# The first FFN of a two-layer diffusion backbone by quarter products, its hidden state through DRAM

## The chip, the cores and the metric

The kernel runs on one core of one Trainium2 chip. The metric is the device time of one execution in microseconds; lower is better. The core has TensorE (matrix products, accumulated in PSUM banks of 512 fp32 columns), VectorE, ScalarE, GpSimd, and DMA queues, all of whose transfers here are issued by SyncE. Each engine works off its own instructions in order and waits on semaphores for the others; so the order of the instructions on an engine, which the tile framework's scheduler sets when it compiles the program, decides what a waiting instruction holds up.

## The reference

Two layers over 1024 latent tokens and 256 context tokens of width 1024. Each layer has a mixer (attention and gating in layer 0, Fourier mixing and a gated linear scan in layer 1), whose result goes through an out projection, and a SwiGLU FFN of hidden width 2816. The change is about layer 0's FFN, which works on tokens and context, and about what stands directly ahead of it and behind it.

```python
# layer 0: ab_mixer, layer 1: cd_mixer; D_MODEL 1024, SEQ 1024, CTX_LEN 256, FFN_HIDDEN 2816, all float32
def swiglu(h, w_gate, w_up, w_down):
    return (jax.nn.silu(h @ w_gate) * (h @ w_up)) @ w_down
...
    for i in range(DEPTH):
...
        mod = (silu_c @ ada_w[i] + ada_b[i])[:, None, :]
        mod_c = (silu_cc @ ada_w[i] + ada_b[i])[None, None, :]
...
        x = x + g_m * y
        x = x + g_f * swiglu(modulate(rmsnorm(x, norm_ffn_w[i]), sh_f, sc_f), ffn_w_gate[i], ffn_w_up[i], ffn_w_down[i])
        if not last:
            ctx = ctx + gc_m * y_c
            ctx = ctx + gc_f * swiglu(modulate(rmsnorm(ctx, norm_ffn_w[i]), shc_f, scc_f),
                                      ffn_w_gate[i], ffn_w_up[i], ffn_w_down[i])
    return rmsnorm(x, final_norm_w)
```

## The kernel before

All matrix products are done in split precision: each fp32 operand is a sum of a high and a low part (`split`, lines 54 to 57: a cast on ScalarE, a subtraction on VectorE), and `mm3` (lines 46 to 51) issues three matmuls, high by high, high by low, low by high. Activations lie transposed, width on the partitions: eight tiles `xT` of 128 x 1280 (tokens 0 to 511 as block 0, 512 to 1023 as block 1, the context as columns 1024 to 1279), and the normed input of the FFN `hT` as pairs named `hh`, `hl`, with `hc` for their context columns. The hidden width is 22 tiles of 128; two of them are a pair.

**Layer 0's FFN** (`ffn`, from line 329) goes over the 22 hidden tiles. `weights` (line 334) loads and splits 1024 x 128 of the gate and of the up matrix. `up` (line 337) makes, block by block, the gates `pg` and ups in PSUM, the product of silu and up (lines 347, 348), and its split `hhi`, `hlo`. After every second tile, `down` (line 352) multiplies two hidden tiles with 256 rows of the down matrix into eight output tiles `dn` per block, each at once added to `xT` by `residual` (line 318), on four PSUM banks in turn (tags t, t, m, o). Gates, ups and downs so alternate, and the hidden state stays on chip. After each `up` a `tick` carries the background generator `ada` (from line 160) one step on: it loads 512 KB of the conditioning weights (`adaw`, with one buffer in this stage) and adds them, scaled, to `adaacc` on VectorE (line 185, 1024 wide); after each eighth load TensorE transposes the sum (`adat`, banks m and o) and VectorE reduces it (line 207).

Ahead of it, `out_proj` (line 767) goes block by block in the order 0, 1, context, loads its weights in four parts for the first block, keeps two parts in the ring and splits two again into other places, and adds each output to `xT`. The rms norm (`rstd` line 266, `norm` line 285) follows block by block: squares on ScalarE, their sum `sqacc`, a sum over the partitions by TensorE (`ss`), a power on GpSimd, a spread over the partitions by TensorE (`rbc`, line 263), eight tiles each of line 297 and, for the low part, line 306.

**Layer 1's FFN** works by quarters for all pairs but the first: `quad` (line 645) takes the tokens and the two tiles of a pair as a 2 x 2 block matrix, and gets the four results from seven products (`qp`) instead of eight, each 4 slices of 128 by 3 matmuls of 512 columns, with sums of `hT` that are made once beforehand (`Sums`, `norm_second`) and sums of weight quarters. `Feed` (line 533) makes the weight units: `quarters` (line 582) loads 2 x 512 KB, subtracts on GpSimd (line 588) and splits units of 512 x 128 into a ring of four. Results are put together by VectorE's adds (line 650). Each pair's gates, the downs of the pair before (`down_sums`, line 745) and its ups alternate. There, `Norm.add` (line 436) makes the squares beside the residuals of `out_proj`, and `norm_first` stands behind block 0.

Between the layers `spill` writes `xT` to DRAM (`xd`), and the next stage begins with products `va`.

## Time and profile before

| | us |
|---|---|
| three runs | 2811.56 to 2816.33, median 2816.05 |
| the profiled execution | 2814.21 |
| its span, first to last instruction | 2812.4 |
| TensorE busy | 2703.8 (96%) |
| VectorE busy | 1739.5 (62%) |
| ScalarE busy | 956.9 (34%) |
| GpSimd busy | 314.7 (11%) |
| layer 0's FFN, first gates to the last pair's downs | 735 to 1621 |
| layer 1's FFN by quarters | 2173 to 2749 |

The profile is of one execution, which took 1.8 us more than its span. Busy time of TensorE is from a matmul's start to its modelled end, and matmuls overlap, so what one costs in a stream is read from the starts in the timeline. TensorE's granted clock was 0.988 of 2.4 GHz in the mean over the span.

### The profile page before, as it was taken

The page shows a single profiled execution, that of the slowest core. Times are in us where ns is not written, and L with a number is a line of the kernel's source. Part 1 is how long each engine was busy: PE and PEld are TensorE (multiplying, and loading weights), DVE is VectorE, ACT ScalarE, POOL GpSimd, SP SyncE. Part 2 cuts the span into 40 slices and gives each one's busy share as a digit, 9 for nine tenths or more (in the row PEclk, how much of TensorE's full clock was granted, in tenths as well). Part 3 has the DMA queues.
Part 4 walks back from the last instruction along what each step waited for, and adds up shares of the span by engine and source line. Part 5 has one row for each costly group of instructions (what it writes and reads, how often), then busy time and mean ns, then how long its engine had stood idle before and what let it go on. Part 6 is the DMA issues. An engine that isn't in the chain of part 4 may idle for free. (4 is left out here: it accounts for less than half of the span.)

```text
span 2812.4 us, 38777 instructions
## 1 busy us (share of the span) xinstructions
PE 2703.8 (96%) x14687; PEld 2295.6 (82%) x14687; DVE 1739.5 (62%) x3090; ACT 956.9 (34%) x2058; POOL 314.7 (11%) x313
## 2 busy tenths in 40 slices
PE   8999899989999999999999999899999999999998
PEld 3889788777888888888888878788777888888887
DVE  5655677666674545546434374866677666667666
ACT  3442466554421111111111145565334222223222
POOL 0000122221100000000000020312002111212111
PEclk9999999999999999999999999999899999999999
DMA  8545655765142322213211143452550211111112
GB/s 307 160 134 154 184 161 160 221 197 168 53 122 66 90 60 83 83 53 98 73 48 45 31 137 104 122 169 65 169 180 24 64 57 45 46 60 53 61 53 83
DMA packets 263162, 298.52 MB, mean 106 GB/s; under 512 B 33416, under 2 KB 206145, under 8 KB 262977
## 3 DMA queue, kind: packets, MB, share of 16 engines
q1 hardware_dynamic: 262977, 296.06, 34.7%
q8 instruction: 116, 1.90, 0.3%
q14 instruction: 69, 0.57, 0.1%
HBM read 228.09 MB, written 64.49 MB: 104 GB/s over the span
## 5 line engine op out<-in xcount | busy, mean ns | idle before, releaser
L56 ACT CAST whi<-wraw 128x512 fp32r<-128x512 f32 (+2 forms) x309 | 235.4, 766 | 722.8 <-PE dn L50 413.9
L318 DVE SCALAR_TENSOR_TENSOR xT<-dn,mod,xT 128x512 f32<-128x512 f32 (+1 forms) x448 | 300.5, 685 | 127.7 <-PE dn L51 126.8
L57 DVE TENSOR_TENSOR wlo<-wraw,whi 128x512 fp32r<-128x512 f32 (+2 forms) x309 | 282.3, 916 | 136.5 <-ACT whi L56 135.1
L49 PE MATMUL dn<-hhi,whi 128*128 128x512 f32 (+1 forms) x896 | 328.0, 367 | 4.9 <-DVE xT L318 3.3
L50 PE MATMUL dn<-hlo,whi 128*128 128x512 f32 (+1 forms) x896 | 326.7, 365 | 0.0
L51 PE MATMUL dn<-hhi,wlo 128*128 128x512 f32 (+1 forms) x896 | 326.5, 365 | 0.0
L49 PE MATMUL pg<-hh,whi 128*128 128x512 f32 x688 | 268.6, 390 | 1.2 <-DVE sg L348 1.2
L51 PE MATMUL pg<-hh,wlo 128*128 128x512 f32 x688 | 268.5, 390 | 0.6 <-DVE wlo L57 0.6
L50 PE MATMUL pg<-hl,whi 128*128 128x512 f32 x688 | 267.9, 389 | 0.0
L185 DVE SCALAR_TENSOR_TENSOR adaacc<-adaw,cs,adaacc 128x1024 f32<-128x1024 f32 x140 | 175.0, 1281 | 112.8 <-DMA adaw<-in_ada_w_dram 110.2
L49 PEld LDWEIGHTS dn<-hhi,whi 128*128 128x128 f32 x896 | 168.9, 189 | 36.9 <-DVE xT L318 8.0
L51 PEld LDWEIGHTS dn<-hhi,wlo 128*128 128x128 f32 x896 | 168.9, 189 | 27.0
L50 PEld LDWEIGHTS dn<-hlo,whi 128*128 128x128 f32 x896 | 169.0, 189 | 26.6
L588 POOL TENSOR_TENSOR wraw<-wraw 128x512 f32<-128x512 f32 x80 | 113.9, 1424 | 499.3 <-DVE wlo L57 293.2
L347 ACT ACTIVATE sg<-pg 128x512 f32<-128x512 f32 (+1 forms) x66 | 34.6, 524 | 353.8 <-PE pg L51 353.8
L348 DVE TENSOR_TENSOR sg<-sg,pg 128x512 f32<-128x512 f32 (+1 forms) x66 | 39.2, 594 | 187.0 <-ACT sg L347 187.0
L51 PEld LDWEIGHTS pg<-hh,wlo 128*128 128x128 f32 x688 | 129.2, 188 | 28.3 <-DVE wlo L57 1.5
L49 PEld LDWEIGHTS pg<-hh,whi 128*128 128x128 f32 x688 | 129.2, 188 | 27.1 <-DVE sg L348 1.4
L50 PEld LDWEIGHTS pg<-hl,whi 128*128 128x128 f32 x688 | 129.2, 188 | 25.9
L277 POOL TENSOR_TENSOR sqacc<-sqacc,sq 128x512 f32<-128x512 f32 (+1 forms) x14 | 17.0, 1218 | 901.5 <-ACT sq L276 900.4
L1058 POOL TENSOR_SCALAR y<-y,sst 128x768 f32<-128x768 f32 (+2 forms) x80 | 71.9, 900 | 257.8 <-DVE sst L1057 129.3
L50 PE MATMUL pg<-hc,whi 128*128 128x256 f32 x344 | 96.8, 281 | 0.0
(653 smaller groups left out, 6644.2 us busy)
## 6 DMA issues: line engine op xcount, KB each, us to landing
adaw<-in_ada_w_dram SPq DMA_DIRECT2D x96, 512.0 KB, 3.8
wraw<-in_ffn_w_gate_dram SPq DMA_DIRECT2D x44, 512.0 KB, 3.6
wraw<-in_ffn_w_up_dram SPq DMA_DIRECT2D x44, 512.0 KB, 3.7
wraw<-in_ffn_w_down_dram SPq DMA_DIRECT2D x44, 512.0 KB, 3.9
wraw<-in_ab_w_in_dram SPq DMA_DIRECT2D x20, 512.0 KB, 5.9
xd<-xT SPq DMA_DIRECT2D x16, 640.0 KB, 6.2
xs<-xd SPq DMA_DIRECT2D x32, 256.0 KB, 3.2
xd<-xs SPq DMA_DIRECT2D x32, 256.0 KB, 3.0
```

What stands on the lines that cost most here:

```text
L49: nc.tensor.matmul(out, wh, xh, start=start, stop=False)
L50: nc.tensor.matmul(out, wh, xl, start=False, stop=False)
L51: nc.tensor.matmul(out, wl, xh, start=False, stop=stop)
L56: s.nc.scalar.copy(hi, src)
L57: (s.nc.gpsimd if eng == "pool" else s.nc.vector).tensor_tensor(lo, src, f32(hi), ALU.subtract)
L185: nc.vector.scalar_tensor_tensor(acc[:, v], w, c, acc[:, v], ALU.mult, ALU.add)
L277: (add or nc.vector).tensor_tensor(acc[:, :n], acc[:, :n], sq[:, :n], ALU.add)
L318: s.nc.vector.scalar_tensor_tensor(xT[k][:, o:o + n], ps, s.mod[l][:, 8 * vec + k, sel:sel + 1], xT[k][:, o:o + n], ALU.mult, ALU.add)
L347: nc.scalar.activation(sg[:, :n], pg[:, :n], AF.Silu)
L348: nc.vector.tensor_tensor(sg[:, :n], sg[:, :n], pu[:, :n], ALU.mult)
L588: sub = lambda out, x, y: feed.s.nc.gpsimd.tensor_tensor(out, x, y, ALU.subtract)
L1058: nc.gpsimd.tensor_scalar(y[:, :256 + xn], y[:, :256 + xn], st[:, 5:6], 1.0, ALU.mult, ALU.mult)
```

## The change

Layer 0's FFN is rewritten to work by quarters, in two phases.

- `out_proj` runs its blocks in the order 0, context, 1. Its weights stay in a ring of three buffers: four loads for the first block, and the first two parts loaded and split again later. Layer 1 uses the same code, so its own order of weights changes too (2, 4, 6, 0 for block 1 instead of 4, 6, 0, 2). `Norm.add` follows each residual. x1 is written to DRAM.
- PSUM changes to single banks for the products. The first hidden pair is multiplied plainly; then the sums are made.
- **Phase 1**: for the ten other pairs a quad of gates and a quad of ups. The context columns are multiplied `beside`, on the same weight units (`cp`, 256 columns); for this a quad has an eighth unit. The hidden pairs, 2.6 MB each, go to DRAM (`hd`), except the last.
- **Phase 2**: x1 is loaded again, into the places that held the sums and inputs, and the downs of all eleven pairs follow, the hidden pairs loaded two pairs ahead.
- The conditioning is done by `ada_half`, with 512-wide loads of 256 KB in two buffers and 112 ticks: 8 a pair in phase 1, 3 a pair in phase 2.
- The scratch ring of the norm has 8 buffers instead of 9, and `norm_second`'s sums reuse a tile.

The diff, cut to its core ("..." marks what is left out):

```diff
+def ada_half(s, a, l, vecs):
+    nc = s.nc
+    for m in vecs:
+        sums = s.adap.tile([P, 2, 8], F32, name="adasum", tag="adasum", bufs=1)
+        for hf in range(2):
+            acc = s.adap.tile([P, 2, 512], F32, name="adaacc", tag="adaacc", bufs=1)
+            for k in range(KT):
+                w = s.adap.tile([P, 512], F32, name="adaw", tag="adaw", bufs=2)
+                c0 = D * m + 512 * hf
+                nc.sync.dma_start(w, a["ada_w"][l, k * P:(k + 1) * P, c0:c0 + 512])
+                for v in range(2):
+                    c = s.cs[:, k, v + 2:v + 3]
+                    if k == 0:
+                        nc.scalar.mul(acc[:, v], w, c)
+                    else:
+                        nc.vector.scalar_tensor_tensor(acc[:, v], w, c, acc[:, v], ALU.mult, ALU.add)
+                if k < KT - 1:
+                    yield 1
+            for v in range(2):
+                pt = psum(s, "mo"[v], "adat")
+                for j in range(4):
+                    nc.tensor.transpose(pt[:, j * P:(j + 1) * P], acc[:, v, j * P:(j + 1) * P], s.ident)
+                nc.vector.tensor_reduce(sums[:, v, 4 * hf:4 * hf + 4], pt.rearrange("p (j q) -> p j q", j=4),
+                                        AX.X, ALU.add)
+            if hf == 0:
+                yield 1
+        nc.vector.tensor_tensor(s.mod[l][:, 8 * m:8 * (m + 1), :], sums.rearrange("p v c -> p c v"),
+                                s.adab[:, 48 * l + 8 * m:48 * l + 8 * (m + 1)].rearrange("p (c o) -> p c o", o=1)
+                                .to_broadcast([P, 8, 2]), ALU.add)
+        yield 1
...
+def norm_ctx(s, N, hT):
+    N.spread()
+    for k in range(KT):
+        N.tile(k, scratch(s)[:, :CT], hT)
...
+def quarters(w, j, ctx=False):
...
-        sub(t, t, b11)
+        if not ctx:
+            sub(t, t, b11)
         for b in (b11, b21):
             feed.unit(b)
+            yield 0
+        if ctx:
+            feed.unit(t)
+            sub(t, t, b11)
             yield 0
         feed.unit(t)
         sub(t, b22, t)
...
+def quad(s, feed, xs, u, out, done, ctx=None):
     nc = s.nc
     add = lambda out, x, y: nc.vector.tensor_tensor(out, x, y, ALU.add)
+    pc = [psum(s, "t", "cp")[:, :CT] for _ in range(2)] if ctx else None
+    def beside(w, x, half):
+        for k in range(4):
+            mm3(nc, pc[x], (w[0][:, k, :], w[1][:, k, :]), ctx[0](4 * half + k), k == half == 0, k == 3 and half == 1)
+        if half:
+            ctx[1](x, pc[x])
     def product(i):
-        hi, lo = feed.take()
+        w = feed.take()
         ps = psum(s, "s", "qp")
         for k in range(4):
-            mm3(nc, ps, (hi[:, k, :], lo[:, k, :]), xs(i, k), k == 0, k == 3)
+            mm3(nc, ps, (w[0][:, k, :], w[1][:, k, :]), xs(i, k), k == 0, k == 3)
+        if ctx and i in (1, 2, 3):
+            beside(w, *{1: (0, 0), 2: (0, 1), 3: (1, 1)}[i])
+        if i in (1, 2, 5, 7):
+            tick(s)
...
+    if ctx:
+        beside(feed.take(), 1, 0)
+        feed.ahead()
...
+        if self.store:
+            for dst, src in zip(self.store[x], self.h[y, x]):
+                self.s.nc.sync.dma_start(dst[:, o:o + n], f32(src))
...
+def down_sums(s, feed, xT, hs, l, blocks, behind=None):
+    order = [(c, y, o, n) for c in (0, 4) for y, (o, n) in enumerate(blocks)]
...
+        if c == 0:
+            tick(s)
...
+    todo = list(zip(blocks, ((0, 2, 4, 6), (2, 4, 6, 0), (4, 6, 0, 2))))
+    steps = [(blk, k0) for blk, ks in todo for k0 in ks]
+    ahead, after = {0: (0, 2, 4)}, {0: (6,), 4: (0,), 8: (2,)}
+    weights = lambda k: wslab(s, w[q0 * P:(q0 + nq) * P, k * P:(k + 2) * P], nq, 2 * P)
+    for i, (blk, k0) in enumerate(steps):
...
+        for k in ahead.get(i, ()):
+            kept[k] = weights(k)
...
+        if i < len(steps) - 2:
+            for k in after.get(i, ()):
+                kept[k] = weights(k)
+        for x in range(2):
+            residual(s, xT, k0 + x, blk, ps[x][:, :n], l, 2)
+            norms[blk].add(k0 + x)
+        if k0 == todo[i // 4][1][-1]:
+            behind(blk)
...
+def load_x1(s, xT, xd, blocks):
+    for o, n in blocks:
+        for k in range(KT):
+            s.nc.sync.dma_start(xT[k][:, o:o + n], xd[k][:, o:o + n])
...
+def load_hidden(s, hd, i):
+    hs = {}
+    for x in range(2):
+        t, c = ([f(s, p, 2 * i + x) for p in range(2)] for f in (hslot, cslot))
+        for p in range(2):
+            s.nc.sync.dma_start(f32(t[p]), hd[x][p][:, :T])
+            s.nc.sync.dma_start(f32(c[p]), hd[x][p][:, T:])
+        for y, (o, n) in enumerate(XBLK):
+            hs[y, x] = [u[:, o:o + n] for u in t]
+        hs[2, x] = c
+    return hs
...
+            place = lambda i, k: slot(s, k if i == 6 else 4 + k, (P, 2, 512), F32R, name="sums")
...
+            def behind(blk):
+                if blk == BLK[0]:
+                    norm_first(s, N[blk], hT, S)
+                    ws.append(early_weights(s, lambda i: ep.tile([P, 2, 512], F32R, name=f"e{i}"), wg))
+                elif blk == BLK[2]:
+                    norm_ctx(s, N[blk], hT)
+                else:
+                    spill(s, xT, xd[0])
+            out_proj(s, a["ab_w_out"][0], mix, xT, 0, [BLK[0], BLK[2], BLK[1]], [4, 5, 6, 7], N, behind)
+            single_banks(s, pps)
+            wps.close()
+            s.wp = wps.enter_context(R("wpf"))
+            fps = es.enter_context(ExitStack())
+            s.fp = fps.enter_context(R("fpf"))
+            pairs = range(2, HT, 2)
+            jobs = [whole(wu, 0)] + [quarters(w, j, True) for j in pairs for w in (wg, wu)]
+            order = [HT - 2] + list(range(0, HT - 2, 2))
+            feed = Feed(s, jobs + [rows(wd, j) for j in order])
+            ws.append(feed_whole(feed))
+            xs = lambda i, k: S.operand(hT, i, k)
+            ctx_ = lambda k: [h[:, T:TA] for h in hT[k]]
+            H = Hidden(s, ctx_, hd[0:2])
+            sums, rest = norm_second(s, N[BLK[1]], hT, S)
+            for y in (0, 2, 1):
+                H.plain(ws, hT, y)
+            sums()
+            rest()
+            nps0.close()
+            eps.close()
+            s.fh = fps.enter_context(R("fhf"))
+            s.adap = fps.enter_context(R("ad1"))
+            s.bg = chain(ada_half(s, a, 0, [5]), ada_half(s, a, 1, range(6)))
+            H.keep_all()
+            for j in pairs:
+                H = Hidden(s, ctx_, hd[j:j + 2] if j < HT - 2 else None)
+                H.gate(feed, xs)
+                H.up(feed, xs)
...
             xT = alloc_x(s)
...
+            load_x1(s, xT, xd[0], BLK)
+            hs = {HT - 2: H.h}
+            for i, j in enumerate(order):
+                for n in (0, 1, 2) if i == 0 else (i + 2,):
+                    if 0 < n < len(order):
+                        hs[order[n]] = load_hidden(s, hd[order[n]:order[n] + 2], n % 4)
+                down_sums(s, feed, xT, hs[j], 0, BLK)
+            drain(s)
+            acol(s, 1, 0)
+            acol(s, 1, 1)
+        wps.close()
+        s.wp = wps.enter_context(R("wp"))
+        double_banks(s, pps)
+        spill(s, xT, xd[1])
+        s.np_ = nps.enter_context(P_("np2", side="left"))
+        hT = alloc_hc(s)
```

On TensorE, in the gates of a later pair: each row is line, instruction, output <- inputs and shape; `hh` and `hl` are the two parts of the input, `whi` and `wlo` of a weight. Before, gates and ups of one block alternate on the same input:

```order
L49 MATMUL pg<-hh_514,whi 128x512
L50 MATMUL pg<-hl_515,whi 128x512
L51 MATMUL pg<-hh_514,wlo 128x512
L49 MATMUL pg<-hh_516,whi 128x512
L50 MATMUL pg<-hl_517,whi 128x512
L51 MATMUL pg<-hh_516,wlo 128x512
L49 MATMUL pg<-hh_516,whi 128x512
L50 MATMUL pg<-hl_517,whi 128x512
L51 MATMUL pg<-hh_516,wlo 128x512
```

After, the last slice of a quarter product `qp` and the first ones of the context product `cp` on the same weight unit:

```order
L51 MATMUL qp<-hh_516,wlo 128x512
L49 MATMUL qp<-hh_518,whi 128x512
L50 MATMUL qp<-hl_519,whi 128x512
L51 MATMUL qp<-hh_518,wlo 128x512
L49 MATMUL cp<-hc_528,whi 128x256
L50 MATMUL cp<-hc_529,whi 128x256
L51 MATMUL cp<-hc_528,wlo 128x256
L49 MATMUL cp<-hc_530,whi 128x256
L50 MATMUL cp<-hc_531,whi 128x256
```

What moved: the context columns, which had a pass of their own behind the two token blocks, now stand between the quarter products.

On VectorE, ahead of the first FFN: line 297 and 306 are the norm's tiles of block 0, line 318 the residuals of the out products `op`. Before, with the residuals of block 1:

```order
L306 SCALAR_TENSOR_TENSOR hl_513<-nt,mod_180,hh_512 128x512
L297 SCALAR_TENSOR_TENSOR nt<-xT_7780,acol_183,rbc 128x512
L297 SCALAR_TENSOR_TENSOR nt<-xT_7781,acol_183,rbc 128x512
L306 SCALAR_TENSOR_TENSOR hl_517<-nt,mod_180,hh_516 128x512
L318 SCALAR_TENSOR_TENSOR xT_7784<-op,mod_180,xT_7784 128x512
L297 SCALAR_TENSOR_TENSOR nt<-xT_7782,acol_183,rbc 128x512
L297 SCALAR_TENSOR_TENSOR nt<-xT_7783,acol_183,rbc 128x512
L318 SCALAR_TENSOR_TENSOR xT_7785<-op,mod_180,xT_7785 128x512
L306 SCALAR_TENSOR_TENSOR hl_521<-nt,mod_180,hh_520 128x512
```

After, where lines 418 and 427 are the norm's tiles and line 351 is the residual, now of the context (256 columns):

```order
L418 SCALAR_TENSOR_TENSOR a_7859<-xT_7782,acol_183,rbc 128x512
L427 SCALAR_TENSOR_TENSOR hl_517<-a_7859,mod_180,hh_516 128x512
L418 SCALAR_TENSOR_TENSOR a_7860<-xT_7783,acol_183,rbc 128x512
L418 SCALAR_TENSOR_TENSOR a_7860<-xT_7784,acol_183,rbc 128x512
L418 SCALAR_TENSOR_TENSOR a_7861<-xT_7785,acol_183,rbc 128x512
L427 SCALAR_TENSOR_TENSOR hl_521<-a_7860,mod_180,hh_520 128x512
L418 SCALAR_TENSOR_TENSOR a_7861<-xT_7786,acol_183,rbc 128x512
L427 SCALAR_TENSOR_TENSOR hl_525<-a_7861,mod_180,hh_524 128x512
L351 SCALAR_TENSOR_TENSOR xT_7783<-op,mod_180,xT_7783 128x256
```

What moved: residuals of the next block stood between the norm's tiles, and now stand behind the last of them; a weight subtraction of 1024 columns (`wlo`) stands just ahead of these tiles.

On TensorE, at the end of the first FFN, where the last pair's downs `dn` meet the next norm (`ss` its sums over the partitions, `rbc` its spread). Before, at block 0's sums:

```order
L51 MATMUL dn<-hhi,wlo 128x512
L50 MATMUL dn<-hlo,whi 128x512
L51 MATMUL dn<-hhi,wlo 128x512
L281 MATMUL ss<-ones,sqacc 128x1 x4
L49 MATMUL dn<-hhi,whi 128x512
L50 MATMUL dn<-hlo,whi 128x512
```

After, where `va` is the first product of the next stage:

```order
L49 MATMUL dn<-hc_15760,whi 128x256
L50 MATMUL dn<-hc_15761,whi 128x256
L51 MATMUL dn<-hc_15760,wlo 128x256
L314 MATMUL ss<-ones,sqacc 128x1 x8
L296 MATMUL rbc<-diag,ones 128x512
L314 MATMUL ss<-ones,sqacc 128x1 x2
L49 MATMUL va<-whi,hh_16449 128x272 x2
```

What moved: the sums and the spread of block 0 stood among the last pair's downs, and now stand behind the last of these, together with those of block 1 and the context (`x8`, `x2`).

## Rows read from the trace of the kernel before

**Rows 1.** Page, part 1: busy us of each engine, share, instructions

```profile
PE 2703.8 (96%) x14687; PEld 2295.6 (82%) x14687; DVE 1739.5 (62%) x3090; ACT 956.9 (34%) x2058; POOL 314.7 (11%) x313
```

**Rows 2.** Windows: busy us by engine, clock, DMA share, GB/s

```profile
735.00:1620.00 885.00, 881.02 (x4658) 758.18 (x4657) 439.44 (x580) 153.30 (x219) 3.84 (x6) 1.00 0.23 70
2173.00:2749.00 576.00, 576.00 (x2543) 476.95 (x2542) 392.61 (x542) 162.02 (x273) 108.78 (x76) 1.00 0.17 54
1621.50:1673.00 51.50, 45.41 (x260) 37.60 (x259) 38.31 (x57) 22.56 (x38) 18.97 (x16) 1.00 0.43 146
...
620.00:650.00 30.00, 26.32 (x163) 22.88 (x164) 21.83 (x66) 16.99 (x51) 5.26 (x7) 1.00 0.74 230
```

**Rows 3.** Waits of TensorE, 735 to 1621: total us, times, longest

```profile
PE dn L49 <- DVE xT L318: 1.4, 3, 0.9
PE pg L49 <- DVE sg L348: 1.2, 1, 1.2
```

**Rows 4.** Timeline of TensorE, 2172.9 to 2179: start us, duration, instruction

```profile
2173.00 0.39 PE L50 MATMUL qp<-mixc,whi 128*128 128x512 f32 x1
...
2175.72 0.39 PE L50 MATMUL qp<-mixd,whi 128*128 128x512 f32 x1
```

**Rows 5.** Timeline of TensorE, 1001.5 to 1004.6

```profile
1001.58 0.28 PE L49 MATMUL dn<-hhi,whi 128*128 128x256 f32 x1
...
1004.45 0.40 PE L49 MATMUL pg<-hh,whi 128*128 128x512 f32 x1
```

**Rows 6.** Groups of VectorE, 735 to 1620: count, busy us, mean ns, idle before

```profile
L185 DVE SCALAR_TENSOR_TENSOR adaacc<-adaw,cs,adaacc 128x1024 f32<-128x1024 f32 x98 | 123.0, 1281 | 99.1 <-DMA adaw<-in_ada_w_dram 98.9
...
L318 DVE SCALAR_TENSOR_TENSOR xT<-dn,mod,xT 128x256 f32<-128x256 f32 x80 | 36.9, 481 | 8.5 <-PE dn L51 8.5
L57 DVE TENSOR_TENSOR hlo<-sg,hhi 128x512 fp32r<-128x512 f32 x44 | 30.4, 690 | 23.4 <-ACT hhi L56 23.4
...
L207 DVE TENSOR_REDUCE adasum<-adat 128x4 f32<-128x512 f32 x28 | 18.6, 684 | 40.1 <-PE adat L206 40.1
...
L348 DVE TENSOR_TENSOR sg<-sg,pg 128x256 f32<-128x256 f32 x21 | 8.7, 414 | 0.0
```

**Rows 7.** Groups of VectorE, 2173 to 2749

```profile
L57 DVE TENSOR_TENSOR wlo<-wraw,whi 128x512 fp32r<-128x512 f32 x173 | 130.4, 754 | 58.5 <-ACT whi L56 57.2
L318 DVE SCALAR_TENSOR_TENSOR xT<-dn,mod,xT 128x512 f32<-128x512 f32 x157 | 117.5, 749 | 67.5 <-PE dn L51 67.4
L650 DVE TENSOR_TENSOR hu<-qp,hu 128x512 f32<-128x512 f32 x57 | 39.3, 689 | 43.3 <-PE qp L51 43.1
...
L738 DVE TENSOR_TENSOR g<-g,g 128x512 f32<-128x512 f32 x9 | 16.0, 1778 | 0.0
L738 DVE TENSOR_TENSOR hu<-hu 128x512 f32<-128x512 f32 x9 | 16.0, 1773 | 0.0
...
L738 DVE TENSOR_TENSOR g<-g,ua 128x512 f32<-128x512 f32 x18 | 12.4, 688 | 0.3
```

**Rows 8.** Group of GpSimd, 2173 to 2749

```profile
L588 POOL TENSOR_TENSOR wraw<-wraw 128x512 f32<-128x512 f32 x76 | 108.8, 1431 | 470.1 <-DVE wlo L57 271.4 <-DMA wraw<-in_ffn_w_up_dram 138.3 <-DMA wraw<-in_ffn_w_gate_dram 36.5
```

**Rows 9.** Waits of VectorE, 735 to 1620

```profile
DVE adaacc L185 <- DMA adaw<-in_ada_w_dram: 98.9, 39, 8.7
...
DVE hlo L57 <- ACT hhi L56: 26.2, 40, 0.7
```

**Rows 10.** Waits of TensorE, 2040 to the end

```profile
PE op L49 <- ACT nt L439: 4.9, 1, 4.9
PE ss L450 <- DVE nt L443: 2.4, 1, 2.4
PE pg L49 <- ACT nt L439: 1.6, 1, 1.6
```

**Rows 11.** Wait of TensorE, 1600 to 1680

```profile
PE rbc L263 <- DVE diag L260: 1.7, 1, 1.7
```

**Rows 12.** DMA issues on the page: count, KB each, us to landing

```profile
adaw<-in_ada_w_dram SPq DMA_DIRECT2D x96, 512.0 KB, 3.8
```

More of the change, by code (lines that the diff above doesn't have):

```diff
@@ L579, in ahead, with feed_whole @@
             next(self.gen, 0)
-def quarters(w, j):
+def feed_whole(feed):
+    units = [[u.rearrange("p k n -> p (k n)") for u in feed.take()] for _ in range(4)]
+    return [[units[2 * half + x] for half in range(2)] for x in range(2)]
+def quarters(w, j, ctx=False):
     loads = [w[512 * x:512 * (x + 1), j * P:(j + 2) * P].rearrange("(k p) n -> p k n", p=P) for x in range(2)]
@@ L1873, in body @@
         nps = ExitStack()
[L1874 to L1896 removed]
+        s.nbanks = "mo"
@@ L1947, in body @@
     feed = Feed(s, jobs + [rows(wd, HT - 2)])
-    units = [feed.take() for _ in range(4)]
-    ws.append([[[u.rearrange("p k n -> p (k n)") for u in units[2 * half + x]] for half in range(2)] for x in range(2)])
+    ws.append(feed_whole(feed))
     H = Hidden(s)
-    sums, rest = norm_second(s, norms_[XBLK[1]], hT, S)
+    sums, rest = norm_second(s, N[XBLK[1]], hT, S)
     H.plain(ws, hT, 0)
@@ L1958, in body @@
     s.fh = pool("fp3", side="right")
-    for y in range(2):
-        for x in range(2):
-            H.keep(y, x)
+    H.keep_all()
     xs = lambda i, k: S.operand(hT, i, k)
@@ L1965, in body @@
         H.gate(feed, xs)
-        down_sums(s, feed, xT, last.h, 1)
+        down_sums(s, feed, xT, last.h, 1, XBLK)
         H.up(feed, xs)
     sps.close()
-    down_sums(s, feed, xT, H.h, 1, final(s, pool("fin", side="left"), a, xT, out))
+    down_sums(s, feed, xT, H.h, 1, XBLK, final(s, pool("fin", side="left"), a, xT, out))
     dump("x4", xT, T)
```

254 lines of the change are left out of this document (95 added, 159 removed).

## The prediction

> **What bounds the kernel now.** I read the page first: TensorE is busy for 96% of the span [rows 1], so the first question is how many matmul columns go away, and the second is where TensorE will wait that does not wait today. The table of windows gives the stages. In the first FFN (735 to 1620 us) TensorE is busy for 881.0 of 885 us and VectorE for half of it; in the second FFN, which already uses quarter products, TensorE never stops while VectorE is at 392.6 of 576 us [rows 2]. The waits of TensorE in the first FFN are a few single microseconds, the longest 1.2 [rows 3]. So the stage is a pure matmul stream, and a matmul that is left out there is saved in full, as long as the work beside it keeps up. What a matmul costs is the step from start to start, not the printed duration (0.39 us, which overlaps): the twelve of 512 columns in the timeline go from 2173.00 to 2175.72 us, 0.2267 us each [rows 4], the 24 of 256 columns from 1001.58 to 1004.45 us, 0.120 us each [rows 5].
>
> **Products removed.** A pair of hidden tiles needs, per matrix, eight block products of 512 columns; by quarters it needs seven. A block product is 4 slices of the contraction by 3 matmuls, 12 matmuls. Ten of the eleven pairs, two matrices: 10 x 2 x 12 = 240 matmuls x 0.2267 = **-54.4 us**. Context columns cost the same 96 matmuls of 256 per pair as before, only spread over the quarter units, and the down products are all kept. A pair's gates and ups then take 168 x 0.2267 + 96 x 0.120 = 49.6 us instead of 55.0, and a pair's downs 96 x 0.2267 + 48 x 0.120 = 27.5 us as before.
>
> **Phase 1, what lies beside.** Per pair VectorE gets 16 unit subtractions, 14 adds, 4 multiplications and 4 hidden subtractions of 512 columns (0.69 us each by [rows 6], 0.69 for an add by [rows 7]), four 256-wide ones at 0.41, 14 accumulations of 512 (half of the 1281 ns of the 1024-wide row) and 2 reductions at 0.684 [rows 6]: 11.0 + 9.6 + 2.8 + 2.8 + 1.7 + 9.0 + 1.4 = 38.2 us. GpSimd also gets 8 subtractions per pair, and in the second FFN VectorE's instructions grow beside these: 173 subtractions of 754 instead of 690 ns, 18 multiplications of 1775 instead of 688 [rows 6, 7], about 33 us over 76 GpSimd instructions [rows 8], 0.43 us each. So 38.2 + 3.4 = 41.6 of 49.6 us, 84%, against 68% in the second FFN and 50% today [rows 2]. That is hidden, but with little slack, and VectorE works in order: an accumulation that waits for its load holds up the adds behind it, and these hold the four single PSUM banks of the products. I take 0.4 us a pair, **+4 us**. Bounds: 0, as in the second FFN where TensorE had no idle time at all, and 2.5 us a pair, 25 us, one wait of VectorE for a load (98.9 us over 39 waits [rows 9]) that comes through uncovered in each pair.
>
> The Trainium skill ("SBUF — State Buffer", section "SBUF: two separate sides") speaks against this change: VectorE's instructions with two SBUF inputs and GpSimd's instructions that read SBUF share a port pair as "an exclusive lock", and the loser waits for the whole instruction. The multiplications of two SBUF tiles at 1.78 us beside ones at 0.69 agree with it; that 754 ns is the mean of the unit subtractions says that most of them do not collide. By the rule at its worst the term is that of the third rival below; by the rows it is the 3.4 us above.
>
> **Phase 2, what lies beside.** Per pair 24 residual steps, 8 x (2 x 0.749 + 0.481) = 15.8 us, 4 unit subtractions at 0.754, 3.0 us, three ticks of the conditioning (six accumulations at 0.64, 3.8 us) and about half a microsecond of reductions: 23.1 of 27.5 us [rows 6, 7]. Downs used to alternate with gates and ups, in which VectorE could catch up; now eleven follow each other, on the four banks that the conditioning's transposes also use. The reloads are 2.6 MB of hidden, 1.0 MB of weights and 0.8 MB of conditioning a pair, 4.4 MB in 27.5 us, 160 GB/s; 230 GB/s was moved where the attention's inputs were loaded [rows 2]. I take 0.4 us a pair, **+4 us**, between 0 and the 2.5 us a pair again, 25 us.
>
> **Between the phases.** x1 comes back into the places that held the sums, so its loads cannot start before the last quad's sixth and seventh products are through. Two products of 2.72 us and some context matmuls lie behind these, some 9 us, and the first block's 2.1 MB need 2.1 / 0.230 = 9 us. The first residuals may come a little late; **+2 us**, bounds 0 and 10 (both the load of the first block and its issue uncovered).
>
> **The seam ahead of the first FFN.** Today VectorE's order mixes the block-1 residuals among the norm's tiles. In the new order the whole first norm and a weight subtraction of 1024 columns stand ahead of the context's last four residuals. The kernel has this order already in layer 1, and there the out products wait 4.9 us for a PSUM pair that such residuals must free [rows 10] (the row names ScalarE; what frees the pair is the residual that runs just ahead of that square). I take that row less what the present seam already loses on a smaller scale: **+4 us**, bounds 0 and 9 (4.9, and the 2.4 and 1.6 us that TensorE waits behind it in that seam, none of which the present seam would then already hold).
>
> **The seam of layer 1.** Its order stays, the wait of 4.9 us with it; a weight subtraction of 1024 columns (1.2 us) joins the norm there. **+1 us**, bounds -5 (the other order of the weights does away with the wait) and +2.
>
> **The tail of the first FFN.** Today the last pair's downs go block by block, and the next norm's sums and first products are mixed into them; from the first of these downs to the last product of block 0 of the next stage it takes 51.5 us [rows 2], with a wait of 1.7 at the norm's broadcast [rows 11]. Now the order is by column half, so block 0 is final only some 8 us ahead of the end, and in TensorE's order all downs, all sums and the broadcast stand ahead of the first product. 27.5 us of downs, 22 us of products and 4 to 5 us of norm in the open make 53 to 55: **+3 us**, bounds -3 and 10.
>
> **The sum**, made against the profiled execution (2814.2 us, of which 2812.4 are the span and 1.8 lie around it): -54.4 + 4 + 4 + 2 + 4 + 1 + 3 = -36.4, so 2777.8. The median of the runs is 1.8 above the profiled execution, which gives 2779.6; I say **2779 us**.
>
> **Rivals.** (1) The four banks and VectorE do not keep up in phase 2: a residual chain that comes late by 2 to 4 us a pair adds 22 to 44 us in place of 4: 2797 to 2819, in the middle 2808. For it: 84% of VectorE with no stage to catch up in, and adat on the downs' banks. Against it: today's downs wait only 1.4 us in all [rows 3]. Chance 0.12.
> (2) The slower side: the conditioning's loads hold up VectorE in phase 1. There are now eight 256 KB loads a pair on SP's queue, behind unit loads and hidden stores that wait in order. If each holds VectorE as long as a wait does today, 98.9 / 39 = 2.5 us [rows 9], VectorE needs 41.6 + 20 = 62 us a pair, 12 more than TensorE: 122 us in all, 2901. It costs something from 1.0 us a load on and makes the kernel slower from 1.5 on (12 us a pair). For it: VectorE's in-order wait is a fact of the rows. Against it: today one buffer serves these loads, and two will; a load lands in 3.8 us [rows 12], half the size now, and a tick comes only every 6 us. Chance 0.07.
> (3) VectorE becomes the bound of phase 1 by collisions: were every one of GpSimd's 8 instructions a full 1.43 us of delay [rows 8], VectorE would stand at 38.2 + 11.4 = 49.6, and its waits for ScalarE at the hidden casts (26.2 us over 40, 0.65 each [rows 9], six a pair) would put it at 53.5, 3.9 over TensorE: 39 instead of 4, 2814, no change. This is the skill's lock taken in full. Chance 0.05.
> (4) The seams and reloads come at their upper bounds together, since x1, hidden and weights stand in one queue: 10 + 9 + 10 instead of 2 + 4 + 3 is +20, 2799. Chance 0.06.
> (5) Nearly nothing is lost: overheads of 5 in place of 18, 2766. Chance 0.05.
>
> **How the numbers follow.** The forecast (2779, by itself 2768 to 2795) has 0.65. What a measurement of this kernel can tell from no change is about 0.2%, 5.6 us, so faster means below 2810.4. The forecast, rivals 4 and 5, most of rival 1 (0.09) and a little of rival 3 give 0.87; the rest of rivals 1 and 3 gives 0.05 for no change; rival 2 and the far ends 0.08 for slower. For eight in ten the range needs the forecast's own, rivals 4 and 5 and the lower half of 1: 2755 to 2808.
>
> **What would show it.** In the changed kernel's windows, a phase-1 pair should take 50 us and a down pair 27.5 to 28; the matmul count should fall by 240. The waits of TensorE in phase 1 should name the product banks (adds of VectorE), not the units; many waits of the adds' chain behind conditioning loads would be rival 2, downs waiting for residuals in phase 2 rival 1, multiplications and unit subtractions far above 0.75 us rival 3. I am wrong if TensorE idles for more than 25 us in the two phases, or if the step of a 512-column matmul is not 0.227 us there.

## The result, and the profile after

The changed kernel takes 2786.07 us in the median of four runs (2782.36 to 2788.42), against 2816.19 for the kernel before: a ratio of 0.9894, 95% interval 0.9877 to 0.9911. A second set of runs on another chip gave 0.9894 again (0.9867 to 0.9920). The prediction was 2779 with a range of 2755 to 2808, so the time lies in the range, 7 us above the forecast. The profiled execution's span is 2785.7 us, 26.7 less than before.

First the engines on the page of the changed kernel, to be held against [rows 1]:

```profile
PE 2656.1 (95%) x14447; PEld 2257.2 (81%) x14447; DVE 1943.0 (70%) x3510; ACT 1024.2 (37%) x2246; POOL 426.8 (15%) x389
```

There are 14447 matmuls where there were 14687: the 240 are gone. VectorE has gone from 62 to 70% of the span, GpSimd from 11 to 15%.

Where the time went is read from the first and last starts of a few products, in the view of one tile (the two numbers ahead of the semicolon are first and last start). The kernel before, its out products of layer 0:

```profile
L49 PE MATMUL op<-hh,whi x48: 387/389/628, 651.4 to 694.1; 128*128 128x512 f32 x48
```

its gates:

```profile
L49 PE MATMUL pg<-hh,whi x688: 387/389/501, 720.0 to 1615.2; 128*128 128x512 f32 x172
```

and its last `va`:

```profile
L51 PE MATMUL va<-cvh,hc x16: 285/288/291, 1724.0 to 1729.7; 128*128 128x272 f32 x16
```

The changed kernel, its out products:

```profile
L49 PE MATMUL op<-hh,whi x64: 389/389/497, 653.7 to 729.9; 128*128 128x512 f32 x64
```

its gates:

```profile
L49 PE MATMUL pg<-hh,e x32: 387/389/799, 732.3 to 788.0; 128*128 128x512 f32 x32
```

its quarter products on the input itself:

```profile
L49 PE MATMUL qp<-hh,whi x320: 387/389/472, 790.1 to 1300.6; 128*128 128x512 f32 x160
```

its downs, the first and layer 0's last:

```profile
L49 PE MATMUL dn<-hhi,whi x416: 277/389/499, 1301.3 to 2773.7; 128*128 128x512 f32 x124, 128*128 128x256 f32 x15
...
L51 PE MATMUL dn<-hc,wlo x160: 276/281/283, 1340.0 to 1608.6; 128*128 128x256 f32 x160
```

and its last `va`, the last product of the stage behind the first FFN:

```profile
L51 PE MATMUL va<-cvh,hc x16: 285/288/291, 1697.3 to 1702.9; 128*128 128x272 f32 x16
```

With the last pair's first down at 1621.52 before and 1580.35 after (timelines of TensorE), and layer 1's marks read in the same way, the span divides as follows (the forecast in the third line is -54.4 for the products and 4 + 4 + 2 for what lies beside them):

| stretch of layer 0 unless said | before, us | after, us | predicted | measured |
|---|---|---|---|---|
| start to first out product | 651.4 | 653.7 | 0 | +2.3 |
| first out product to first gate product | 68.6 | 78.6 | +4 | +10.0 |
| first gate product to the last pair's downs | 901.5 | 848.1 | -44.4 | -53.4 |
| last pair's downs to the last `va` | 108.2 | 122.6 | +3 | +14.4 |
| that to layer 1's first out product | 334.0 | 332.5 | 0 | -1.5 |
| layer 1: first out to first gate product | 62.7 | 64.3 | +1 | +1.6 |
| the rest | 686.0 | 686.0 | 0 | 0.0 |

So the products saved came in almost in full, and two thirds of what the three seams cost (26.0 us for 8) were not foreseen. The first line is within the scatter of runs: the same code stands at 650.5 in the second profile of this kernel, and between 650.7 and 654.4 in the experiments below.

The waits of TensorE from the out projection to the mixer of layer 1 (total us, times, longest) name the two seams and not the two phases:

```profile
PE va L49 <- ACT whi L56: 7.5, 1, 7.5
PE op L49 <- ACT nt L395: 6.5, 1, 6.5
PE ss L314 <- POOL sqacc L310: 6.1, 2, 3.6
...
PE qp L49 <- ACT whi L56: 2.0, 1, 2.0
PE rbc L296 <- DVE diag L293: 1.9, 1, 1.9
PE qp L49 <- DVE hu L626: 1.7, 4, 0.5
```

The stretches of the two phases, to be held against [rows 2] (busy us of TensorE, its weight loads, VectorE, ScalarE, GpSimd; then clock, DMA share, GB/s), and the stretch of the tail:

```profile
790.00:1301.00 511.00, 506.13 (x2720) 436.77 (x2720) 395.65 (x592) 178.69 (x327) 116.57 (x80) 1.00 0.43 142
1301.00:1610.00 309.00, 307.68 (x1627) 264.91 (x1625) 239.99 (x384) 37.41 (x63) 6.25 (x5) 1.00 0.46 162
1580.40:1673.00 92.60, 75.17 (x466) 67.31 (x466) 63.15 (x104) 39.86 (x76) 18.81 (x18) 0.87 0.42 136
```

In phase 1 TensorE is busy for 506.1 of 511 us with VectorE at 395.7 (77%), in phase 2 for 307.7 of 309 with VectorE at 240.0 (78%). In the tail its clock is down to 0.87 of 2.4 GHz in the mean.

The groups of VectorE in phase 1, against [rows 6, 7]:

```profile
L231 DVE SCALAR_TENSOR_TENSOR adaacc<-adaw,cs,adaacc 128x512 f32<-128x512 f32 x141 | 125.2, 911 | 16.0 <-DMA adaw<-in_ada_w_dram 15.3
L57 DVE TENSOR_TENSOR wlo<-wraw,whi 128x512 fp32r<-128x512 f32 x161 | 115.2, 723 | 88.9 <-ACT whi L56 88.8
...
L742 DVE TENSOR_TENSOR g<-g,ua 128x512 f32<-128x512 f32 x20 | 20.3, 1015 | 0.3
```

the first two of them in phase 2, where GpSimd is nearly idle:

```profile
L231 DVE SCALAR_TENSOR_TENSOR adaacc<-adaw,cs,adaacc 128x512 f32<-128x512 f32 x55 | 40.4, 743 | 1.2 <-DMA adaw<-in_ada_w_dram 1.2
L57 DVE TENSOR_TENSOR wlo<-wraw,whi 128x512 fp32r<-128x512 f32 x42 | 27.1, 682 | 0.0
```

GpSimd's subtractions in phase 1:

```profile
L558 POOL TENSOR_TENSOR wraw<-wraw 128x512 f32<-128x512 f32 x80 | 116.6, 1457 | 404.3 <-DVE wlo L57 370.4 <-DMA hd_h<-hhi 29.8 <-DVE acol L252 2.6
```

The accumulation of 512 columns takes 743 ns, not half of the 1281 of the 1024-wide one, and 911 where GpSimd subtracts beside it; the last multiplication has gone from 688 to 1015. The excess over the lone prices, 141 x 0.168 + 161 x 0.041 + 20 x 0.327 = 36.8 us over 80 GpSimd instructions, is 0.46 us each, where 0.43 was taken.

### The profile page after: what moved, and what is told of

The parts are those of the page before. It is cut to its first block, busy times and chain, and to the rows that moved or that the text cites. A ratio compares the mean times of both kernels' runs of the same rounds, so it can differ in the third digit from the quotient of the medians.

```text
span 2785.7 us, 39975 instructions
## 1 busy us (share of the span) xinstructions
PE 2656.1 (95%) x14447; PEld 2257.2 (81%) x14447; DVE 1943.0 (70%) x3510; ACT 1024.2 (37%) x2246; POOL 426.8 (15%) x389
## 4 chain that ended last, share of the span: by engine, by line
PE 71%; DVE 12%; DMA 5%; ACT 5%; issue 4%; POOL 2%; SPq 1%; DVEq 0%; POOLq 0%; ACTq 0%
PE qp L49 7%; PE qp L50 7%; PE qp L51 7%; PE dn L49 6%; PE dn L50 6%; PE dn L51 6%; DVE wlo L57 2%; DMA adaw<-in_ada_w_dram 2%; PE o L1141 2%; DVE adaacc L231 2%; PE pt L1111 1%; PE pg L49 1%; PE pg L51 1%; PE pg L50 1%; ACT whi L56 1%
## 5 line engine op out<-in xcount | busy, mean ns | idle before, releaser
L231 DVE SCALAR_TENSOR_TENSOR adaacc<-adaw,cs,adaacc 128x512 f32<-128x512 f32 x196 | 165.6, 864 | 17.3 <-DMA adaw<-in_ada_w_dram 16.5
L49 PE MATMUL dn<-hhi,whi 128*128 128x512 f32 (+1 forms) x416 | 157.2, 378 | 0.0
L51 PE MATMUL dn<-hhi,wlo 128*128 128x512 f32 (+1 forms) x416 | 156.8, 377 | 0.0
L50 PE MATMUL dn<-hlo,whi 128*128 128x512 f32 (+1 forms) x416 | 156.7, 377 | 0.0
L49 PE MATMUL qp<-hh,whi 128*128 128x512 f32 x320 | 125.3, 392 | 4.0 <-ACT whi L56 2.0
L49 PE MATMUL dn<-hslot,whi 128*128 128x512 f32 x320 | 124.8, 390 | 1.2 <-DVE xT L351 1.2
L51 PE MATMUL qp<-sums,wlo 128*128 128x512 f32 x320 | 125.1, 391 | 0.9 <-DVE wlo L57 0.9
L50 PE MATMUL dn<-hslot,whi 128*128 128x512 f32 x320 | 124.7, 390 | 0.0
L51 PE MATMUL dn<-hslot,wlo 128*128 128x512 f32 x320 | 124.7, 390 | 0.0
L51 PE MATMUL qp<-hh,wlo 128*128 128x512 f32 x320 | 124.6, 389 | 0.0
L50 PE MATMUL qp<-sums,whi 128*128 128x512 f32 x320 | 124.6, 389 | 0.0
L49 PE MATMUL qp<-sums,whi 128*128 128x512 f32 x320 | 124.5, 389 | 0.0
L49 PEld LDWEIGHTS dn<-hhi,whi 128*128 128x128 f32 x416 | 78.3, 188 | 14.7 <-ACT hhi L56 0.3
```

The costliest lines, as they stand in the source:

```text
L49: nc.tensor.matmul(out, wh, xh, start=start, stop=False)
L50: nc.tensor.matmul(out, wh, xl, start=False, stop=False)
L51: nc.tensor.matmul(out, wl, xh, start=False, stop=stop)
L231: nc.vector.scalar_tensor_tensor(acc[:, v], w, c, acc[:, v], ALU.mult, ALU.add)
```

## The tail: where the 14 us are

The timeline of the changed kernel at the end of the last downs (start us, duration, instruction; in brackets the idle time ahead and what ended it). VectorE:

```profile
1609.87 0.16 DVE L283 TENSOR_SCALAR rv<-ss 128x4 f32<-128x4 f32 x1 [0.44 <-PE ss L314]
1615.89 1.21 DVE L293 TENSOR_TENSOR diag<-ident,rv 128x512 f32<-128x512 f32 x1 [5.87 <-POOL rv L284]
```

GpSimd:

```profile
1605.28 8.05 POOL L310 TENSOR_TENSOR sqacc<-sqacc,sq 128x512 f32<-128x512 f32 x6 [0.74 <-ACT sq L309]
...
1614.84 1.02 POOL L284 TENSOR_TENSOR rv<-rv,half_neg 128x4 f32<-128x4 f32 x1
```

ScalarE:

```profile
1627.91 1.38 ACT L338 ACTIVATE hh<-nt,mod 128x512 fp32r<-128x512 f32 x2 [1.48 <-DVE nt L330]
1629.20 1.08 ACT L56 CAST whi<-wraw 128x1088 fp32r<-128x1088 f32 x1
```

TensorE:

```profile
1608.62 0.28 PE L51 MATMUL dn<-hc,wlo 128*128 128x256 f32 x1
...
1617.16 2.08 PE L296 MATMUL rbc<-diag,ones 128*128 128x512 f32 x2 [1.91 <-DVE diag L293]
...
1630.33 0.82 PE L49 MATMUL va<-whi,hh 128*128 128x272 f32 x2 [7.49 <-ACT whi L56]
...
1632.39 0.43 PE L51 MATMUL va<-whi,hl 128*128 128x272 f32 x1
1632.61 0.43 PE L49 MATMUL va<-whi,hh 128*128 128x272 f32 x1
```

The last down starts at 1608.6, the first product of the next stage at 1630.3: 21.7 us in which TensorE does next to nothing. Block 0's variance is there at 1609.9, but the power that follows is GpSimd's, and GpSimd first finishes six adds of block 1's squares (8.05 us) and one of the context's; so VectorE waits 5.87 us, of which 1.02 are the power itself. Then come the spread and eight tiles of block 0, one after the other; the cast of the next stage's weights (1629.2) stands behind six of them in ScalarE's order. And when the products begin, they step at 0.22 us for 272 columns (1632.39 to 1632.61): TensorE's granted clock, the column behind the busy times, is 0.50 there, the lower level of 1.2 GHz, 0.74 in the mean of the next 4 us, and 1.00 from 1638 us on.

```profile
1612.00:1630.00 18.00, 4.96 (x14) 3.21 (x14) 9.55 (x16) 7.91 (x15) 9.70 (x11) 0.51 0.42 120
1630.50:1634.00 3.50, 2.66 (x11) 2.34 (x12) 3.50 (x5) 1.71 (x2) 0.00 (x0) 0.50 0.20 36
1634.00:1638.00 4.00, 4.00 (x26) 4.00 (x26) 2.62 (x4) 1.83 (x2) 0.00 (x0) 0.74 0.91 247
1638.00:1642.00 4.00, 4.00 (x34) 4.00 (x34) 1.78 (x2) 1.10 (x1) 0.00 (x0) 1.00 0.49 136
```

Four runs took this apart. In the first, all sums of squares behind the first FFN go to VectorE:

```diff
-        cd_values(s, a, hT, vd, norms(s, xT, hT, 1, 0))
+        cd_values(s, a, hT, vd, lambda blk: norm(s, xT, hT, 1, 0, blk, rstd(s, xT, blk)))
```

> The sums of squares of the norm behind the first FFN are added on VectorE for all three blocks; nothing else changes. In the changed kernel TensorE stands for 21.5 us between the last down product (1608.8) and the first product of the next stage (1630.3), and GpSimd adds block 1's squares (8.05 us) ahead of block 0's power, on which VectorE waits 5.9 us. Theory (the norms pile up, GpSimd's queue first): this gap falls by 4 to 7 us, the kernel to about 2780. Rival (the gap is set by the next stage's weights, loaded behind the spill): the gap stays within 1 us, TensorE's wait for the weights' cast grows instead, 2786.

Its downs of layer 0, first and last start:

```profile
L51 PE MATMUL dn<-hc,wlo x160: 276/281/286, 1344.9 to 1614.1; 128*128 128x256 f32 x160
```

and its products `va`:

```profile
L49 PE MATMUL va<-whi,hh x64: 283/287/563, 1628.9 to 1670.8; 128*128 128x272 f32 x64
...
L51 PE MATMUL va<-cvh,hc x16: 285/288/291, 1695.2 to 1700.8; 128*128 128x272 f32 x16
```

VectorE's wait for the power falls from 5.87 us to 0.9:

```profile
DVE diag L293 <- POOL rv L284: 0.9, 1, 0.9
```

The gap falls from 21.7 to 14.8 us (1614.1 to 1628.9), and from the last down to the last `va` it is 86.7 instead of 94.3. The whole kernel is at 0.9886 (0.9871 to 0.9900), 2787.8 us on a chip where the kernel before takes 2820: too little to tell from the changed kernel's 0.9894. The expectation holds for the stretch, and what GpSimd's queue costs there is shown; for the whole time it is inconclusive.

In the second the spill of x2 is issued behind the next stage's weight loads:

```diff
-        spill(s, xT, xd[1])
         s.np_ = nps.enter_context(P_("np2", side="left"))
...
+        def pre(blk):
+            if blk == BLK[0]:
+                spill(s, xT, xd[1])
+            norms(s, xT, hT, 1, 0)(blk)
```

> The spill of x2 to DRAM is issued behind the next stage's four weight loads instead of ahead of them. The first product waits 7.5 us for the cast of the weights in the changed kernel. Rival (weights come late): the loads are issued some 3 us earlier or more, the cast comes earlier, and the gap of 21.5 us falls by 3 to 7 us, the kernel to about 2781. Theory (the cast stands in ScalarE's order behind the norm's tiles, which are late themselves): less than 1.5 us, 2785 to 2786.

The gap falls here too, to 14.3 us (1615.7 to 1630.0), which is the rival's number; but the stretch to the last `va` is 91.2, only 3.1 less, and the kernel is where it was, 0.9897 (0.9882 to 0.9911). The cast now stands behind two of the norm's tiles instead of six, so the first two products start earlier; the third then waits 2.6 us, where it waited 0.8, for the low part of the weights, which VectorE makes among the tiles, and later products wait 5.8 us in all for ScalarE instead of 3.0. So both hold in part: the cast was late in ScalarE's order for its load's sake, and what VectorE and ScalarE have to do besides was late by itself.

In the third the last pair's downs go block by block, as in the kernel before, and each block's sums stand in the program right behind its downs:

```diff
+    if last:
+        order = [(c, y, o, n) for y, (o, n) in enumerate(blocks) for c in (0, 4)]
...
+        if last and c:
+            last((o, n))
...
+            def last(blk):
+                r[blk] = rstd(s, xT, blk, None if blk == BLK[0] else nc.gpsimd, (s.cp, BLK.index(blk)))
```

> The last pair's down products go block by block (0, 1, context), as in the kernel before, and each block's sum of squares, partition sum and power stand in the program right behind its downs, so that TensorE's order has the sums of blocks 0 and 1 among the downs. Theory (the gap is the three norms that begin only when all downs are done): the gap of 21.5 us falls to 8 to 11 us, what the spread, two tiles and their casts need; the kernel at 2774 to 2777. Rival (weights): the gap stays above 18 us, 2784 or more.

It came out at 0.9976 (0.9966 to 0.9987), 2813.5 us, some 23 more than the changed kernel would take there. The gap is 16.7 us, between the 8 to 11 of the theory and the 18 of the rival; but the downs of phase 2 take 10 us longer, and layer 1's FFN, which the edit doesn't touch, takes 697 instead of 686 us from its first gate product on. Its quarter products last up to 399 ns in the median of the records instead of 389. The edit had put 96 bytes a partition of new tiles into the first SBUF pool; the section on the hardware below has the run that separates the two. With the powers kept in an unused tile, and all sums on VectorE, nothing moves. Against the run before, cut to its core:

```diff
...
-                s.hc.tile([P, 16], F32, name="pad")
+                s.hcpad = s.hc.tile([P, 16], F32, name="pad")
...
-                r[blk] = rstd(s, xT, blk, None if blk == BLK[0] else nc.gpsimd, (s.cp, BLK.index(blk)))
+                r[blk] = rstd(s, xT, blk, None, (s.hcpad, BLK.index(blk)))
```

> As the early sums (last downs by blocks, each block's sum of squares, partition sum and power right behind its downs), with the powers kept in an unused tile, so that nothing moves in SBUF, and all sums on VectorE. In TensorE's order the spread of block 0 still stands behind all downs, and the spread of block 1, whose input VectorE makes after block 0's tiles, ahead of the first product of the next stage. Theory (place in SBUF cost the first try its 20 us, the order of the two spreads keeps the gap open): 389 ns for the products, the gap between the last down and the first product still 13 to 18 us instead of 21.5, the kernel at 0.985 to 0.989 of before. Rival (early sums are dear in themselves): 0.994 or more.

This gives 0.9884 (0.9868 to 0.9900), the gap 15.6 us (1610.7 to 1626.3), the stretch to the last `va` 88.7, as the theory has it. VectorE's sums without the earlier place gave 14.8 and 86.7, so the earlier sums gained nothing on top of them: block 0's spread still stands behind all downs in TensorE's order, and block 1's spread, which needs VectorE behind block 0's tiles, ahead of the first product; TensorE waits 8.0 us for it. A version with the spread among the downs too was not tried.

## The two out projections

Every third pair of out products takes the two PSUM banks of tag t, which there only the last few transposes and products of the mixers still use:

```diff
-        ps = [psum(s, "s", "op") for _ in range(2)]
+        ps = [psum(s, "t" if i % 3 == 2 else "s", "op") for _ in range(2)]
```

> Every third pair of out products takes the two PSUM banks that lie idle there, so three pairs are in turn instead of two; in both layers. Theory (the 6.5 us wait in each out projection is for a pair that residuals behind the norm's tiles free late): both waits of 6.5 us go or fall below 2, -8 to -12 us in all, 2774 to 2778; the stretch from the first out product to the first gate product falls from 78.6 to 72 to 74 us. Rival (the norm's chain on VectorE is what the first gate product waits for anyhow): the waits move to the sums, the spread or the first gate products, less than 3 us, 2783 to 2786.

The kernel is at 0.9834 (0.9817 to 0.9850), 2773.0 us beside 2820.2 for the kernel before: a clear gain over the changed kernel. First to first, out to gate products, layer 0 takes 69.4 instead of 78.6 us and layer 1 54.5 instead of 64.3: 19 us, more than the 8 to 12 expected, though one wait of 3.2 us is left in layer 0 where less than 2 was. The waits of TensorE in layer 0's seam, in the run with three pairs:

```profile
PE op L49 <- DVE xT L351: 3.2, 1, 3.2
```

and in layer 1's:

```profile
PE pg L49 <- ACT nt L395: 1.7, 1, 1.7
PE op L49 <- ACT nt L395: 1.3, 1, 1.3
```

against the changed kernel's 6.5 (above) and, in layer 1:

```profile
PE op L49 <- DVE xT L351: 8.0, 2, 6.5
PE pg L49 <- ACT nt L395: 1.7, 1, 1.7
```

So the pair that residuals behind the norm's tiles free late is what both seams wait for in the main; with a third pair the first seam is nearly back at the 68.6 us that it had in another order before.

## How much slack phase 1 has

One buffer for the conditioning's loads instead of two:

```diff
-                w = s.adap.tile([P, 512], F32, name="adaw", tag="adaw", bufs=2)
+                w = s.adap.tile([P, 512], F32, name="adaw", tag="adaw", bufs=1)
```

> One buffer instead of two for the conditioning's loads. A load then starts only when the two accumulations on the one before are done, so VectorE waits for each. Theory (VectorE has some 10 us of 51 to spare per pair and the product banks cover a wait of 2 us): VectorE's waits for these loads grow from 15 to 18 us in all to 100 to 200, TensorE's waits in phase 1 from about 5 to 9 us to 15 to 40, the kernel 0.992 to 1.000 of before. Rival (VectorE's waits are covered by slack): phase 1 longer by less than 5 us, 0.989 to 0.991.

The waits in phase 1, of VectorE with two buffers:

```profile
DVE adaacc L231 <- DMA adaw<-in_ada_w_dram: 15.3, 18, 2.4
```

with one, of VectorE:

```profile
DVE adaacc L231 <- DMA adaw<-in_ada_w_dram: 51.5, 32, 2.5
```

and of TensorE:

```profile
PE qp L51 <- DVE wlo L57: 18.9, 20, 2.1
```

VectorE waits 51.5 us where it waited 15.3, less than the 100 expected; TensorE's waits go to 18.9, within the 15 to 40, phase 1 from 511 to 517 us (in all other runs) to 531.5, the kernel to 0.9956 (0.9942 to 0.9971). So 36 us more of waits on VectorE cost the end about 17: the mechanism of the prediction's second rival is there, and the second buffer keeps it small.

## Both gains together

> The two edits that gained, together: three pairs of PSUM banks in the out products and all sums of squares on VectorE behind the first FFN. Their places lie apart (at 650 to 735 and 2035 to 2100 us; at 1600 to 1705 us). Theory: the gains add, the out projections' 9 and 10 us and some 5 to 7 us of the tail, 0.980 to 0.982 of the kernel before. Rival (a later wait takes the tail's gain back): as with the banks alone, 0.983 to 0.984.

> The kernel with both edits again, on the chip of the run beside it, so that the two are compared there: 0.980 to 0.983 of the kernel before.

The first pair of edits, banks and VectorE's sums, gives 0.9813 (0.9798 to 0.9828), 2762.9 us, as the theory has it, and on the last chip 0.9806 (0.9785 to 0.9827). With the spill moved as well:

> The kernel with three pairs of banks and all sums on VectorE, and in addition the spill of x2 issued behind the next stage's weight loads. With the sums out of GpSimd's queue the first product of the next stage still starts 14.6 us behind the last down, 7.3 of them a wait of that product. Theory (the norm's tiles and the cast behind them, not the load, are what it waits for): the gap falls by less than 3 us, the kernel stays within 0.2% of the one without this edit. Rival (with the queue gone, the late weight load is next): the gap falls by 4 to 7 us, 0.979 of the kernel before.

0.9795 (0.9770 to 0.9819), 2761.1 us beside 2763.3 without it on the same chip. The gap falls from 14.5 to 8.0 us, the rival's size, and the stretch to the last `va` from 86.4 to 83.4, so again most of the earlier start is waited away; on the whole time the two can't be told apart. These are the fastest versions seen, some 25 us ahead of the changed kernel.

> The changed kernel again, beside the others on one chip. Theory: 0.988 to 0.991 of the kernel before; the stretch from the first quarter product to the first down, 511 us in the first profile and 516 us in three edits that do not touch it, is 511 to 517 us: if 516 here, the spread is of chips and runs, not of the edits.

The changed kernel's phase 1 took 513.7 us there, between its first 511.2 and the 516 to 517 of the edits on another chip. The kernel with two of these edits together, VectorE's sums and the banks, took 513.9 on this chip and 511.2 on another: a spread of chips and runs, not of the edits. The runs of the table are from several chips, so whole times are compared by the ratio.

| run | us (median) | of before | out to gate products, layer 0 | phase 1 | last down to last `va` | out to gate products, layer 1 |
|---|---|---|---|---|---|---|
| changed kernel | 2786.1 | 0.9894 | 78.6 | 511.2 | 94.3 | 64.3 |
| the same, second set | 2788.2 | 0.9894 | 79.0 | 513.7 | 94.2 | 63.9 |
| sums on VectorE | 2787.8 | 0.9886 | 78.4 | 516.2 | 86.7 | 65.9 |
| spill behind the loads | 2790.6 | 0.9897 | 79.7 | 516.9 | 91.2 | 63.5 |
| early sums, 96 bytes moved | 2813.5 | 0.9976 | 79.3 | 515.7 | 92.1 | 64.0 |
| early sums, nothing moved | 2786.6 | 0.9884 | 78.8 | 513.2 | 88.7 | 62.9 |
| three pairs of banks | 2773.0 | 0.9834 | 69.4 | 516.4 | 93.6 | 54.5 |
| one conditioning buffer | 2807.8 | 0.9956 | 78.3 | 531.5 | 94.2 | 63.2 |
| 96 bytes alone | 2807.8 | 0.9961 | 78.4 | 514.0 | 93.8 | 63.2 |
| banks and sums | 2762.9 | 0.9813 | 70.8 | 511.2 | 85.9 | 54.5 |
| banks, sums and spill | 2761.1 | 0.9795 | 70.7 | 513.0 | 83.4 | 54.5 |

## Why the prediction was right, and where it was off

**The products removed: right.** 240 matmuls fewer by the count, and the step of 512 columns is 0.2267 us in both kernels. The forecast said that the stage was a pure stream, and the FFN from its first gates to its last pair fell by 53.4 us, against 54.4 for the products alone.

**What lies beside in the phases: too dear.** The three terms of 4, 4 and 2 us came to 1. The pair period was 51.1 us in phase 1 (511.2 / 10) and 27.9 in phase 2 (279.0 / 10), where 50 and 27.5 to 28 were said to show it right; of the 1.5 above 49.6 some 1.0 are the transposes of the conditioning (80 in phase 1, 10.4 us), which both kernels have and the sum leaves out. TensorE's waits in phase 1 were 4.6 us (5 to 9 in the repeats), on units and on adds, and in phase 2 one of 1.2. That VectorE would be near 84% was near enough (77%); the share of collisions per GpSimd instruction was right, at 0.46 us for 0.43, the price of the 512-wide accumulation was not (0.743 for 0.64). By its own rows the forecast's "about 33 us" of collisions is 30.6 (173 x 0.064 and 18 x 1.087), 0.40 an instruction, which changes nothing in the sum. The third rival, every GpSimd instruction a full delay, did not come: the mean excess is a third of the 1.46 us that such an instruction takes here. The Trainium skill ("SBUF — State Buffer", section "SBUF: two separate sides") says that whichever instruction starts first holds the shared port pair to its end and the other is blocked; single multiplications of 1.35 us in phase 1 and up to 1.78 in layer 1, beside ones of 0.68, agree with that.

**The seam ahead of the FFN: the mechanism right, the size wrong.** +10.0 instead of +4, past the upper bound of 9. The wait was named (a PSUM pair that residuals behind the norm's tiles free) and priced by [rows 10] at 4.9 us, less a little for what the seam lost already. It took 6.5 us, and what failed was to leave the waits around it out of the term: in the stretch from the first out product to the first gate product TensorE waits 11.4 us in all, where it waited 3.1 before. The lower granted clock goes with that, 0.93 in the mean of the stretch instead of 0.98. The run with three pairs takes 9.2 us back.

**Layer 1's seam: right**, +1.6 for +1: the wait of 4.9 us grew to 6.5, and that of 2.4 for the sums went.

**The tail: the step that failed.** +14.4 for +3, past its bound of 10. The order of the downs by column half was seen, and that nothing of the norm would stand among the downs; what failed is the term of 4 to 5 us for the norm in the open. No row of the prediction shows it, and the wait that it names, 1.7 us [rows 11], is one under cover. In the open TensorE stands for 21.7 us, of which 5.9 are VectorE's wait for GpSimd, whose queue the sum did not walk through.

The mark of this term was misread as well. The 51.5 us [rows 2] end with the first 96 products of block 0, not with its last, and the "22 us of products" are these 96, some 12 us, and 10 us of waits, sums and spread that were there already. Before:

```profile
1621.52 0.39 PE L49 MATMUL dn<-hhi,whi 128*128 128x512 f32 x1
...
1672.93 0.29 PE L51 MATMUL va<-whi,hl 128*128 128x272 f32 x1
```

The same marks after:

```profile
1580.35 0.39 PE L49 MATMUL dn<-hslot,whi 128*128 128x512 f32 x1
...
1645.57 0.28 PE L51 MATMUL va<-whi,hl 128*128 128x272 f32 x1
```

So 51.4 became 65.2 us instead of 53 to 55: 28.3 of downs, 21.7 without products, and 15.2 of products. The products were put 7 us too high and the norm 17 too low. Nothing of the 13.8 us came back by the last `va`, where it is 14.4.

**The rivals.** None came true as a whole. The fourth, the seams at their bounds, is the nearest: the two seams were past theirs, but the reloads between the phases cost nothing, and so the time was 2786 and not 2799. The errors, 9 us too dear in the phases and 18 too cheap at the seams, came to 10 in the span (-26.7 for -36.4) and 7 in the median. That the forecast is only 7 us off is so in part luck: two errors of opposite sign.

## What to carry to other kernels

A cost that lies under cover in the profile cannot be read off as the wait that is left there: when an edit takes the cover away, walk through the whole chain on each engine's queue, and look for what stands ahead in the in-order queues (here GpSimd's sums ahead of a power, and ScalarE's tiles ahead of a cast). A wait for a PSUM buffer that an already changed part of the same kernel shows is best taken at its full row for the same structure elsewhere, with the smaller waits behind it. And a seam is the cheap place for gains: two nearly idle PSUM banks gave back more than a quarter of what 240 matmuls were worth.
